# Hybrid decoder layer, the MLP's first matrix in quarters 1 to 3: seven half products in place of eight chunks

## The chip, the cores and the metric

The program runs on one core of one Trainium2 chip. The metric is device time in microseconds for one launch: the median of three runs is given, and one more execution is recorded by the hardware profiler. TensorE multiplies matrices, VectorE (DVE) and ScalarE (ACT) work element by element, GpSimd (POOL) and SyncE (SP) here mostly issue transfers, and 16 DMA engines carry them.

## The reference, cut to what matters

The layer computes a mixer, then an MLP, then a gated embedding. The MLP is

```python
u = rmsnorm(x, norm_mlp_g[i]) @ w_up[i]        # (512, 1024) @ (1024, 4096)
x = x + jnp.square(jax.nn.relu(u)) @ w_down[i] # (512, 4096) @ (4096, 1024)
```

All data are float32. Every product of two matrices is made of three products on TensorE: each factor is split into a high part, which is the factor rounded to the type fp32r, and a low part, the remainder; high by high, high by low and low by high are added in PSUM.

## The kernel before, in words

The 4096 hidden channels of the MLP are worked off in four quarters of 1024. In a quarter `up` makes the hidden values, transposed (channels on partitions, 512 tokens along the free dimension), and `down` multiplies them by the quarter's rows of the second matrix and adds the result to the residual rows `xk`.

`up` makes eight chunks of 128 channels. A chunk loads 512 KB of `w_up` into a buffer `wr`, forms its two parts `wh` and `wl` (`load_w`, `split`: a cast on ACT, then a subtraction on DVE), and runs 24 matmuls of 512 columns (8 slices of the inner dimension, three products each) into one PSUM bank `psg`. ACT applies relu and square. Two chunks give one tile `F` with the four blocks A21, A11, A22, A12 (two channel slices by two halves of the tokens) and four sums of them, S1 to S4, made on DVE. `F` is split into two tiles `uf`, high and low.

`down` is already made in Winograd's way: of the eight half products of a 2 by 2 block product it makes seven, from sums of the blocks on either side. Eight loads of 512 KB give the blocks b11, b12, b21, b22 for each half of the inner dimension; DVE makes sums of them in place; each of 14 forms is split and used in 12 matmuls of 512 columns into one of three PSUM pairs X, Y, Z (`psp`). The same seven products with 256 columns per matmul are used far earlier in the program, where the branch gates are projected (`gate_proj`; 24 matmuls per product).

The parts `wh` and `wl` each have four buffers (`WB = 4`), in rotation over the whole program: the parts of a product can be written as soon as the fourth product before it is done. `wr` has four buffers, `wd` (the first blocks of `down`) six, `F` one.

Another way of splitting stands in the program and is used for activations: `split_by_transfer` casts the high part on ACT, writes the negated high part into the low tile by a second ACT instruction with scale -1, and adds the source to it by an accumulating transfer between two places of SBUF, issued from POOL. DVE has no part in it.

```python
    def split_by_transfer(dst, src):
        A.copy(dst[0], src)
        A.activation(dst[1], src, AF.Copy, scale=-1.0)
        nc.gpsimd.dma_start(out=r32(dst[1]), in_=src, accum_op=ALU.add)
```

A scheduler places the instructions of each engine in one fixed order, by the order of the code and by when it reckons that their operands are there. On the chip each engine works its own list off in that order, and an instruction that waits on a semaphore holds up all that stands behind it.

## Time and profile before

| what | value |
|---|---|
| median of 3 runs | 879.4 us (878.7 to 879.86) |
| the profiled execution's own time | 878.13 us |
| its span, first to last instruction | 876.3 us |
| TensorE busy | 864.2 us (99%) |
| DVE busy | 671.5 us (77%) |
| ACT busy | 490.4 us (56%) |
| MLP, on the chain | 486.3 to 810.0 us |

The profile records one execution. "Busy" is the share of the span in which an engine has an instruction running; a matmul's own duration overlaps the next one's, so the pace of TensorE is read from the starts, not from the mean duration. The chain of waits is followed back from the last instruction: a stretch named PE in it is time in which TensorE itself sets the pace. Line numbers are those of the kernel before unless the text says otherwise.

### The profile page before, as it was taken

How to read it: one execution, taken by the hardware profiler on the slowest of the kernel's cores; microseconds unless marked ns; L12 is line 12 of the kernel's file. 1: busy time of each engine (PE TensorE's matmuls, PEld its weight loads, DVE VectorE, ACT ScalarE, POOL GpSimd, SP SyncE). 2: the span in 40 equal slices, each digit the busy share in tenths (PEclk: the TensorE clock that was granted, in tenths of full speed). 3: DMA queues.
4: the chain of work that ended last, by engine and by line, in shares of the span. 5: the costliest groups of instructions: out<-in, count | busy, mean ns of one | idle time of the engine just before them, and what ended most of it. 6: DMA issues, size and time to landing. Idle time of an engine off the chain costs nothing.

```text
span 876.3 us, 11735 instructions
## 1 busy us (share of the span) xinstructions
PE 864.2 (99%) x4428; PEld 727.1 (83%) x4428; DVE 671.5 (77%) x994; ACT 490.4 (56%) x826; POOL 43.7 (5%) x70
## 2 busy tenths in 40 slices
PE   9999999999999999999999999999999999999996
PEld 7888789998877778888888888888888888888886
DVE  6999889775788889777896669757956784698557
ACT  6685556444676568854344665356435634564843
POOL 1121111000000000000020000000000000020000
PEclk9999999999999999999999999999999999999999
DMA  8775246435121266664244612520452054125302
GB/s 268 209 185 207 97 148 209 146 115 202 49 97 50 72 231 215 209 254 148 73 88 148 222 47 73 204 106 4 135 178 73 0 192 145 49 54 139 120 1 96
DMA packets 35162, 115.14 MB, mean 131 GB/s; under 512 B 4893, under 2 KB 4893, under 8 KB 35106
## 3 DMA queue, kind: packets, MB, share of 16 engines
q1 hardware_dynamic: 28146, 95.25, 31.5%
q0 software_dynamic: 6816, 18.89, 7.9%
q8 instruction: 35, 0.57, 0.3%
q10 hardware_dynamic: 144, 0.26, 0.1%
q14 instruction: 21, 0.17, 0.1%
HBM read 97.60 MB, written 10.49 MB: 123 GB/s over the span
## 4 chain that ended last, share of the span: by engine, by line
PE 84%; DVE 7%; ACT 4%; DMA 3%; issue 2%; SPq 0%; ACTq 0%; DVEq 0%
PE psg L175 47%; PE psp L175 23%; PE psa L175 5%; DVE wl L138 2%; PE pst L175 2%; PE pst L778 1%; ACT wh L137 1%; DMA wr<-in_w_vsif 1%; DMA wq<-in_w_o 1%; ACT lm L743 1%; PE psa L720 1%; PE psa L859 1%; PE psa L881 1%; DVE qs L429 1%; PE psa L879 1%
## 5 line engine op out<-in xcount | busy, mean ns | idle before, releaser
L137 ACT CAST wh<-wr 128x1024 fp32r<-128x1024 f32 x130 | 136.5, 1052 | 159.4 <-PE psg L175 61.7
L138 DVE TENSOR_TENSOR wl<-wr,wh 128x1024 fp32r<-128x1024 f32 x130 | 158.1, 1219 | 79.9 <-ACT wh L137 78.9
L175 PE MATMUL psg<-x,wh 128*128 128x512 f32 x512 | 157.7, 389 | 0.0
L175 PE MATMUL psp<-wh,uf 128*128 128x512 f32 x448 | 138.5, 389 | 0.0
L175 PEld LDWEIGHTS psg<-x,wh 128*128 128x128 f32 x512 | 96.1, 188 | 19.9
L175 PE MATMUL psg<-x,wl 128*128 128x512 f32 x256 | 99.6, 389 | 0.0
L175 PEld LDWEIGHTS psp<-wh,uf 128*128 128x128 f32 x448 | 84.1, 188 | 17.4
L175 PE MATMUL psp<-wl,uf 128*128 128x512 f32 x224 | 87.1, 389 | 0.0
L175 PE MATMUL psg<-h,wh 128*128 128x512 f32 x256 | 80.9, 395 | 0.6 <-DVE rc L746 0.6
L137 ACT CAST wh<-wd 128x1024 fp32r<-128x1024 f32 x44 | 46.2, 1052 | 54.1 <-PE psp L175 21.9
L138 DVE TENSOR_TENSOR wl<-wd,wh 128x1024 fp32r<-128x1024 f32 x44 | 53.1, 1218 | 14.6 <-ACT wh L137 14.5
L175 PEld LDWEIGHTS psg<-x,wl 128*128 128x128 f32 x256 | 48.1, 188 | 9.9
L175 PEld LDWEIGHTS psg<-h,wh 128*128 128x128 f32 x256 | 46.9, 188 | 11.2 <-issue 1.6
L175 PE MATMUL psg<-h,wl 128*128 128x512 f32 x128 | 50.5, 395 | 0.0
L138 DVE TENSOR_TENSOR uf<-F,uf 128x1792 fp32r<-128x1792 f32 (+2 forms) x20 | 33.0, 1652 | 21.8 <-ACT uf L137 21.8
L175 PEld LDWEIGHTS psp<-wl,uf 128*128 128x128 f32 x224 | 42.1, 188 | 8.9
L175 PE MATMUL psg<-yb,wh 128*128 128x512 f32 x128 | 40.3, 393 | 0.0
L175 PE MATMUL psg<-ya,wh 128*128 128x512 f32 x128 | 39.9, 391 | 0.0
L137 ACT CAST uf<-F 128x1792 fp32r<-128x1792 f32 (+2 forms) x20 | 27.9, 1396 | 20.5 <-DVE F L1191 20.4
L1215 DVE SCALAR_TENSOR_TENSOR xk<-psp,r,xk 128x512 f32<-128x512 f32 x48 | 33.8, 744 | 5.5 <-PE psp L175 5.2
L175 PE MATMUL psg<-hS,wh 128*128 128x256 f32 x192 | 35.6, 285 | 0.2 <-DVE t L646 0.2
L175 PE MATMUL psa<-h,wh 128*128 128x256 f32 x192 | 35.4, 285 | 0.3 <-ACT p L656 0.2
(343 smaller groups left out, 1828.4 us busy)
## 6 DMA issues: line engine op xcount, KB each, us to landing
wr<-in_w_up SPq DMA_DIRECT2D x32, 512.0 KB, 3.3
wd<-in_w_down SPq DMA_DIRECT2D x24, 512.0 KB, 4.0
wr<-in_w_qsw SPq DMA_DIRECT2D x8, 512.0 KB, 4.2
gd<-gr POOLq DMA_DIRECT2D x8, 512.0 KB, 2.9
wr<-in_w_qkml SPq DMA_DIRECT2D x8, 512.0 KB, 3.2
wr<-in_w_b SPq DMA_DIRECT2D x8, 512.0 KB, 3.2
wh<-in_w_b POOLq DMA_DIRECT2D x8, 512.0 KB, 3.7
gl<-gd SPq DMA_DIRECT2D x8, 512.0 KB, 4.3
```

The source lines that it names most:

```text
L137: A.copy(dst[0], src)
L138: last_low[0] = V.tensor_sub(dst[1], src, r32(dst[0]))
L175: last_mm[0] = T.matmul(ps, l, r, start=first and i == 0, stop=last and i == len(ops) - 1, skip_group_check=parts)
L429: V.tensor_sub(t[o, :], ps[s, :], r32(t[s, :]))
L720: T.matmul(o, q[:, n * P : (n + 1) * P], kk[kp][ab][:, k0 : k0 + 256], start=True, stop=False)
L743: A.activation(lm3[:, g, :], lm3[:, g, :], AF.Exp, bias=nmx[:, g : g + 1], scale=0.125, accum_out=sm[:, g : g + 1])
L778: T.matmul(o[HALF[ab], :], v[:, c : c + 64], w[:, ab * 512 : (ab + 1) * 512], start=j == 0, stop=j == len(terms) - 1)
L859: T.matmul(psc[s], l, r, start=j == 0, stop=j == 2, skip_group_check=True)
L879: T.matmul(o, hi, vm[s][:, h, :], start=s == 0, stop=False, skip_group_check=True)
L881: last_mm[0] = T.matmul(o, lo, vm[s][:, h, :], start=False, stop=s == t, skip_group_check=True)
L1215: V.scalar_tensor_tensor(o, ps[:, t, :], r2[:, 2 * toks + t : 2 * toks + t + 1], o, ALU.mult, ALU.add)
```

## The change

Quarter 0 keeps its eight chunks (`up`). In quarters 1 to 3 `up_seven` takes their place. It works in two groups of 512 channels. A group loads four blocks of 512 KB (`four`, `_groups` lays `w_up` out for it), and makes seven products into three PSUM pairs, each of 24 matmuls with 256 columns: A11, A12, S2, S1, S3, S4, A22, named for the block or sum of the activations in it. Five sums of the weight blocks are made in place on DVE. The three forms for A11, A12 and S2 are split as before; the four for S1, S3, S4 and A22 are split by transfer. The seven results are put together on DVE with one copy `kept` of A11, then relu and square follow on ACT. The tile `F` now holds one whole group (two channel tiles) in one buffer, and S3 is written over A21.

The sums of the activations (S1 to S4 of x1) are made once, during quarter 0's `up`, on DVE and ACT (`x1_sums`). In `down`, the forms for S3, A22 and S4 are split by transfer in quarters 1 and 2 (`BY_DMA`); its blocks use four `wd` and four `wr` buffers, shared in turn with `up_seven`, and its first loop does the work of both halves one after the other. The scratch for transfer descriptors is set to 8192 bytes.

```diff
--- before.py
+++ after.py
...
+BY_DMA = (1, 2)
...
-    def load_w(src, n, dims, raw=None, cast=False):
+    def load_w(src, n, dims, raw=None, cast=False, how=None):
...
-            split(parts, raw[:, :n])
+            (how or split)(parts, raw[:, :n])
...
-    F = lambda: mp.tile([P, 8, 256], F32, tag="F", bufs=1, name=nm("F"))
-
-    A21, A11, A22, A12, S1, S2, S3, S4 = range(8)
+    F = lambda: mp.tile([P, 2, 7, 256], F32, tag="F", bufs=1, name=nm("F"))
+
+    A21, A11, A22, A12, S1, S2, S4 = range(7)
+    S3 = A21
...
+    def four(src, first):
+        tiles = []
+        for i in range(4):
+            if first:
+                t = np_.tile([P, 1024], F32, tag="wd", bufs=4, name=nm("wd"))
             else:
                 t = wp.tile([P, 1024], F32, tag="wr", bufs=WRB, name=nm("wr"))
-            nc.sync.dma_start(out=t, in_=w_down[q * 8 + c])
-            raws.append(t)
-        return raws
+            nc.sync.dma_start(out=t, in_=src[i])
+            tiles.append(t)
+        return tiles
...
+        q = {n: [r32(t) for t in v] for n, v in quad.items()}
+        add, sub = ALU.add, ALU.subtract
+        s1 = total((q["21"][0], add, q["22"][0]), (add, q["21"][1]), (add, q["22"][1]))
+        s2 = total((s1, sub, q["11"][0]), (sub, q["11"][1]))
+        parts("S2", s2)
+        s3 = total((q["11"][0], sub, q["21"][0]), (add, q["11"][1]), (sub, q["21"][1]))
+        parts("S3", s3)
+        s4 = total((q["12"][0], sub, s2), (add, q["12"][1]))
+        parts("S4", s4)
+
+        def last():
+            split(quad["21"], s1)
+            xsum["S1"] = x1_of(0, 0)
+            xsum["A11"], xsum["A12"], xsum["A22"] = x1_of(0, 256), x1_of(4, 256), x1_of(4, 0)
+
+        return last
...
+    def sums_of(f, cols):
+        V.tensor_add(f[S1], f[A21], f[A22])
+        V.tensor_sub(f[S2], f[S1], f[A11])
+        V.tensor_sub(f[S4], f[A12], f[S2])
+        V.tensor_sub(f[S3], f[A11], f[A21])
...
+    def up_seven(q, uf):
+
+        for g in range(2):
+            c = 8 + ((q - 1) * 2 + g) * 4
+            b11, b12, b21, b22 = four(w_up[c : c + 4], g == 0)
+            X, Y, Z = [pair()[:, :, :256] for _ in range(3)]
+            both = F()
+            f = [both[:, :, i, :] for i in range(7)]
+            kept = mp.tile([P, 2, 256], F32, tag="kp", bufs=1, name=nm("kp"))
+            hl = [new_uf() for _ in range(2)]
+
+            def form(raw, how=None):
+                return load_w(None, 1024, 4, raw, how=how)
+
+            def prod(ps, name, w, first, last):
+                for t in range(2):
+                    ops = []
+                    for k in range(4):
+                        ops += pairs([h[:, k, t * P : (t + 1) * P] for h in w], xsum[name][k])
+                    chain(ps[:, t, :], ops, first, last, True)
+
+            prod(X, "A11", form(b11), True, False)
+            A.copy(kept, X)
+            V.tensor_sub(b12, b22, b12)
+            V.tensor_add(b11, b12, b11)
+            prod(X, "A12", form(b21), False, True)
+            squared(f[A11], X)
+            V.tensor_sub(b21, b21, b11)
+            prod(Z, "S2", form(b11), True, False)
+            V.tensor_sub(b11, b22, b11)
+            V.tensor_add(f[A21], Z, kept)
+            prod(Z, "S1", form(b11, split_by_transfer), False, False)
+            V.tensor_add(f[A22], Z, kept)
+            prod(Y, "S3", form(b12, split_by_transfer), True, False)
+            V.tensor_add(f[A22], Y, f[A22])
+            squared(f[A22], f[A22])
+            prod(Z, "S4", form(b22, split_by_transfer), False, True)
+            V.tensor_add(f[A12], Z, kept)
+            squared(f[A12], f[A12])
+            if g:
+                for t in range(2):
+                    split([h[:, 256 : 4 * 256] for h in hl[t]], flat(both[:, t], 1, 4))
+            prod(Y, "A22", form(b21, split_by_transfer), False, True)
+            V.tensor_add(f[A21], Y, f[A21])
+            squared(f[A21], f[A21])
+            sums_of(f, 512)
+            for t in range(2):
+                if g:
+                    split([h[:, 4 * 256 :] for h in hl[t]], flat(both[:, t], 4, 7))
+                    split([h[:, :256] for h in hl[t]], flat(both[:, t], 0, 1))
+                else:
+                    split(hl[t], flat(both[:, t], 0, 7))
+                uf.append(hl[t])
...
-        raws = load_down(q)
+        raws = four(w_down[q * 8 : q * 8 + 4], True) + four(w_down[q * 8 + 4 : q * 8 + 8], False)
         b11, b12, b21, b22 = [[raws[4 * kh + i] for kh in range(2)] for i in range(4)]
         X, Y, Z = pair(), pair(), pair()
-
-        def form(raw):
-            return load_w(None, 1024, 2, raw)
+        by_dma = split_by_transfer if q in BY_DMA else None
+
+        def form(raw, how=None):
+            return load_w(None, 1024, 2, raw, how=how)
...
-            prod(Y, S3, form(b12[kh]), kh, False, False)
+            prod(Y, S3, form(b12[kh], by_dma), kh, False, False)
         acc(Y, 0, 1)
         for kh in range(2):
             V.tensor_sub(b11[kh], b22[kh], b11[kh])
             prod(Z, S1, form(b11[kh]), kh, True, False)
         acc(Z, 0, 1)
         for kh in range(2):
-            prod(Y, A22, form(b21[kh]), kh, False, True)
+            prod(Y, A22, form(b21[kh], by_dma), kh, False, True)
         acc(Y, 0, 0)
         for kh in range(2):
-            prod(Z, S4, form(b22[kh]), kh, False, True)
+            prod(Z, S4, form(b22[kh], by_dma), kh, False, True)
...
-        up(q, uf)
+        (up_seven if q else up)(q, uf)
...
-        "w_up": _t_form(i["w_up"][0]),
+        "w_up": np.concatenate([_t_form(i["w_up"][0][:, :1024]), _groups(i["w_up"][0][:, 1024:])], axis=0),
...
-    nc = _bacc.Bacc("TRN2", target_bir_lowering=False, num_devices=1)
+    nc = _bacc.Bacc("TRN2", target_bir_lowering=False, num_devices=1, dynamic_dma_scratch_size=8192)
```

Two places of the program show what the change makes of the order. The first is VectorE where quarter 2's `up` begins. In these rows `wl<-wd` or `wl<-wr` is the low part of a weight form, L1215 adds a product of `down` to the residual. Before:

```order
L138 TENSOR_TENSOR wl_6050<-wr_6047,wh_6049 128x1024
L1215 SCALAR_TENSOR_TENSOR xk_4163<-psp_5799,r_4939,xk_4163 128x512
L1215 SCALAR_TENSOR_TENSOR xk_4164<-psp_5799,r_4939,xk_4164 128x512
L138 TENSOR_TENSOR wl_6085<-wr_6082,wh_6084 128x1024
L138 TENSOR_TENSOR wl_6127<-wr_6124,wh_6126 128x1024
L1215 SCALAR_TENSOR_TENSOR xk_4165<-psp_5800,r_4939,xk_4165 128x512
L1215 SCALAR_TENSOR_TENSOR xk_4166<-psp_5800,r_4939,xk_4166 128x512
L138 TENSOR_TENSOR wl_6162<-wr_6159,wh_6161 128x1024
L138 TENSOR_TENSOR wl_6204<-wr_6201,wh_6203 128x1024
```

After, at the same place (L1275, L1276, L1279 and L1281 are the sums of the weight blocks, `wd_6256` to `wd_6262` the first group's b11, b12, b21, b22, `wr_6501` the second group's b12, L1327 the addition to the residual, `wl_6305` the low part for A12 and `wl_6336` that for S2, L1282 the first use of a result):

```order
L1275 TENSOR_TENSOR wd_6258<-wd_6262,wd_6258 128x1024
L139 TENSOR_TENSOR wl_6305<-wd_6260,wh_6304 128x1024
L1276 TENSOR_TENSOR wd_6256<-wd_6258,wd_6256 128x1024
L1275 TENSOR_TENSOR wr_6501<-wr_6505,wr_6501 128x1024
L1327 SCALAR_TENSOR_TENSOR xk_4165<-psp_6004,r_4939,xk_4165 128x512
L1327 SCALAR_TENSOR_TENSOR xk_4166<-psp_6004,r_4939,xk_4166 128x512
L1279 TENSOR_TENSOR wd_6260<-wd_6260,wd_6256 128x1024
L139 TENSOR_TENSOR wl_6336<-wd_6256,wh_6335 128x1024
L1281 TENSOR_TENSOR wd_6256<-wd_6262,wd_6256 128x1024
L1282 TENSOR_TENSOR F_6267<-psp_6266,kp_6268 128x2x256
```

Where the splits of independently loaded chunks stood between the additions, there now stand sums that feed each other. The source of the form for S1 is written by L1281; the second group's b12, both additions and the split for S2 stand ahead of it.

The second place is ScalarE in the second group of quarter 2. Before, in the middle of that quarter's `up` (relu, square, the cast of a chunk, and the cast of `F`):

```order
L1174 ACTIVATE rt_6112<-psg_6081 128x512
L1178 ACTIVATE F_6079<-rt_6112 128x512
L137 CAST uf_6115<-F_6079 128x1792
L137 CAST wh_6280<-wr_6278 128x1024
L1174 ACTIVATE rt_6154<-psg_6123 128x512
L1178 ACTIVATE F_6156<-rt_6154 128x512
L137 CAST wh_6315<-wr_6313 128x1024
L1174 ACTIVATE rt_6189<-psg_6158 128x512
L1178 ACTIVATE F_6156<-rt_6189 128x512
L137 CAST uf_6192<-F_6156 128x1792
```

After, from the last relu and square of the first group on (`wh_6608` and `wl_6609` are the two parts for the second group's S1, `wh_6638` and `wl_6639` those for its S3, `kp` the copy of A11, `uf` the cast of the first group's `F`, L147 the copy with scale -1 after which the transfer can be issued):

```order
L1219 ACTIVATE F_6267<-F_6267 128x2x256
L1220 ACTIVATE F_6267<-F_6267 128x2x256
L146 CAST wh_6608<-wr_6499 128x1024
L1274 COPY kp_6511<-psp_6507 128x512
L147 ACTIVATE wl_6609<-wr_6499 128x1024
L146 CAST wh_6638<-wr_6501 128x1024
L138 CAST uf_6269<-F_6267 128x1792
L147 ACTIVATE wl_6639<-wr_6501 128x1024
L138 CAST uf_6271<-F_6267 128x1792
```

The copy of A11 and one cast of `F` now stand between the casts and the scaled copies of S1 and S3.

More of the change, by code (lines that the diff above doesn't have):

```diff
@@ L1167, in up @@
         for f in range(8):
-            if q == 0 and f < 2:
+            if f < 2:
                 ps = begun[f]
@@ L1179, in up @@
-            if q == 0 and f == 2:
+            done = squared(flat(fs, o, o + 2), ps)
+            if f == 2:
                 with tc.issue_after(done.ins):
                     squares()
+                    last = x1_sums()
             if f % 2:
-                hl = [np_.tile([P, 7 * 256], F32R, tag="uf", bufs=8, name=nm("uf")) for _ in range(2)]
-                cut = 3 * 256 if f == 7 else 0
-                if cut:
-                    split([t[:, :cut] for t in hl], fs[:, 1:4, :].rearrange("p a b -> p (a b)"))
-                V.tensor_add(fs[:, S1, :], fs[:, A21, :], fs[:, A22, :])
-                V.tensor_sub(fs[:, S3, :], fs[:, A11, :], fs[:, A21, :])
-                V.tensor_sub(fs[:, S2, :], fs[:, S1, :], fs[:, A11, :])
-                V.tensor_sub(fs[:, S4, :], fs[:, A12, :], fs[:, S2, :])
-                split([t[:, cut:] for t in hl], fs[:, 1 + cut // 256 :, :].rearrange("p a b -> p (a b)"))
-                uf.append(hl)
+                hl = new_uf()
+                if f == 7:
+                    split([t[:, 256 : 4 * 256] for t in hl], flat(fs, 1, 4))
+                sums_of([fs[:, i, :] for i in range(7)], 256)
+                if f == 7:
+                    split([t[:, 4 * 256 :] for t in hl], flat(fs, 4, 7))
+                    split([t[:, :256] for t in hl], flat(fs, 0, 1))
+                else:
+                    split(hl, flat(fs, 0, 7))
+                uf.append(hl)
@@ L1228, in down @@
             V.tensor_sub(b12[kh], b22[kh], b12[kh])
-        for kh in range(2):
             w = form(b11[kh])
```

46 lines of the change are left out of this document (33 added, 13 removed).

## The prediction, made blind

> **What bounds the kernel now.** I read the page first, then the chain of waits, the waits of TensorE, and the busy time by stage.
>
> ```profile
> span 876.3 us, 11735 instructions
> ...
> PE 864.2 (99%) x4428; PEld 727.1 (83%) x4428; DVE 671.5 (77%) x994; ACT 490.4 (56%) x826; POOL 43.7 (5%) x70
> ...
> PEclk9999999999999999999999999999999999999999
> ```
>
> TensorE is busy in nearly the whole span, at full clock in every slice. The chain says how tightly:
>
> ```profile
> 176.61 2.88 PE psa L175 x24
> 179.49 2.88 PE psg L175 x24
> ...
> 565.20 43.52 PE psg L175 x192
> 608.72 38.08 PE psp L175 x168
> 646.80 43.52 PE psg L175 x192
> 690.32 38.08 PE psp L175 x168
> 728.40 43.52 PE psg L175 x192
> 771.92 38.11 PE psp L175 x168
> ```
>
> Columns are start, length, and number of instructions. Each `up` is one stretch of 43.52 us, each `down` one of 38.08 us, with nothing between. A 512-column matmul costs 43.52/192 = 0.2267 us, so a half product of `down` (12) takes 2.72 us. The first two rows are the gate projection, the same seven products with 256 columns: 24 matmuls in 2.88 us, 0.120 us each, a little over half.
>
> ```profile
> PE psg L267 <- DVE zero L215: 1.1, 1, 1.1
> ...
> 122.00:203.00 81.00, 80.44 (x665) 79.21 (x664) 66.02 (x89) 42.72 (x52) 7.33 (x13) 1.00 0.44 157
> ...
> 646.80:690.30 43.50, 43.50 (x193) 36.03 (x193) 25.30 (x29) 21.55 (x26) 0.00 (x0) 1.00 0.22 74
> 690.30:728.40 38.10, 38.10 (x170) 31.56 (x169) 33.09 (x35) 17.50 (x18) 0.00 (x0) 1.00 0.40 138
> ```
>
> The first row is TensorE's longest wait of the run, 1.1 us at the start. The others are stretches: window, length, then busy PE, PEld, DVE, ACT, POOL, clock, DMA share. In quarter 2's `up` DVE (25.3 of 43.5 us) and ACT (21.6) have room; in `down` DVE has little (33.1 of 38.1). The gate projection kept TensorE full (80.4 of 81) with ACT half idle and no transfers in its splits.
>
> **The change, part by part.** Prices, from the groups and the transfer views:
>
> ```profile
> L137 ACT CAST wh<-wr 128x1024 fp32r<-128x1024 f32 x130 | 136.5, 1052 | 159.4 <-PE psg L175 61.7 <-PE psp L175 48.0 <-issue 17.3
> L137 ACT CAST uf<-F 128x1792 fp32r<-128x1792 f32 x12 | 20.3, 1696 | 18.8 <-DVE F L1191 18.8
> L1178 ACT ACTIVATE F<-rt 128x512 f32<-128x512 f32 x32 | 20.3, 633 | 7.4 <-DVE uf L138 6.8
> L1174 ACT ACTIVATE rt<-psg 128x512 f32<-128x512 f32 x32 | 18.9, 589 | 1.2 <-PE psg L175 1.2
> L882 ACT COPY hs<-psa 128x512 f32<-128x512 f32 x8 | 4.3, 575 | 2.2 <-PE psa L881 2.2
> L1150 ACT ACTIVATE junk<-xk 128x1024 f32<-128x1024 f32 x4 | 4.2, 1046 | 0.0
> ...
> L138 DVE TENSOR_TENSOR wl<-wr,wh 128x1024 fp32r<-128x1024 f32 x130 | 158.1, 1219 | 79.9 <-ACT wh L137 78.9 <-PE psg L175 0.8
> L1215 DVE SCALAR_TENSOR_TENSOR xk<-psp,r,xk 128x512 f32<-128x512 f32 x48 | 33.8, 744 | 5.5 <-PE psp L175 5.2
> L138 DVE TENSOR_TENSOR uf<-F,uf 128x1792 fp32r<-128x1792 f32 x12 | 24.3, 2025 | 21.8 <-ACT uf L137 21.8
> L747 DVE TENSOR_TENSOR lm<-lm,rc 128x512 f32<-128x512 f32 x16 | 11.0, 689 | 0.4
> L1232 DVE TENSOR_TENSOR wd<-wd,wd 128x1024 f32<-128x1024 f32 x8 | 9.7, 1217 | 0.0
> L648 DVE TENSOR_TENSOR t<-psa,t 128x512 f32<-128x512 f32 x8 | 5.5, 686 | 1.4 <-PE psa L175 1.4
> ...
> DMA  0000089979999999999999996000000000000007
> ...
> q0 software_dynamic: 864, 1.57, 52.9%
> ...
> wr<-in_w_up SPq DMA_DIRECT2D x32, 512.0 KB, 3.3
> ...
> hS<-s POOLq DMA_DIRECT2D x8, 256.0 KB, 4.2
> ...
> DMA to landing us min/median/max: 3.2/4.2/7.4
> ...
> DMA to landing us min/median/max: 3.3/5.5/7.5
> ```
>
> *TensorE's saving.* An `up` goes from 192 x 0.2267 = 43.52 us to 14 x 2.88 = 40.32 us: 3.2 us a quarter, 9.6 us in all. That is the whole gain.
>
> *Work that must hide.* Per group TensorE has 7 x 2.88 = 20.2 us. ACT gets 7 casts (7.4), 4 scaled copies (4.2, by the 1.046 of an ACTIVATE of that size), the copy of A11 (0.6), 4 relus and squares (4.9), 2 casts of `F` (3.4): 20.5 us. DVE gets 5 sums (6.1), 3 splits (3.7), 5 additions from PSUM (3.4), 4 sums of `F` (2.8), 2 splits of it (4.1): 20.1 us. Both are as full as TensorE, with lists in fixed order; a wait of one is not made up inside the group.
>
> *The price of a remainder by transfer.* The last two rows are 256 KB adding transfers (L147, and `xk<-p1s` of L1225): 3.2 and 3.3 us from issue to landing when least disturbed. The DMA row above them covers 783 to 800 us in 40 slices of 0.425 us: six such transfers fill 20 slices, 1.4 us each. The change moves 512 KB, not shown here: 3.3 + 1.4 = 4.7 us alone, and up to 7.5 + 1.4 = 8.9 in a queue. I take L = 5.0, near the low end, since the gating ones are issued singly. Each also needs cast and scaled copy, 2.1 us: 7.1 us against 3 x 2.88 = 8.6 us from a buffer's release to its use. It fits only if ACT starts at once.
>
> *Start of quarters 2 and 3* (time 0 = end of the preceding `down`). A form there may begin when the product four earlier is done. S4's first transfer waits for S1's first half, which ends 5 x 2.72 = 13.6 us before 0; + 2.1 + 5.0 = -6.5. Only then may b22 be loaded into that buffer: + 3.3 = -3.2. DVE then works its row: b12 -2.0, split for A12 -0.8, b11 0.4, the second group's b12 1.7, two additions 3.1, b21 4.4, split for S2 5.6, source of S1 6.8. ACT: cast 7.9, relu of A12's result (queued ahead) 8.5, scaled copy 9.5; landing at 14.5. TensorE reaches the first matmul that needs it at 3 x 2.88 + 0.24 = 8.9. **Wait 5.6 us**, twice = 11.2. In quarter 1 no transfer delays the loads: additions 1.5, split for S2 2.7, source 3.9, scaled copy 6.0, landing 11.0 against 9.1: 1.9.
>
> *Second group* (0 = end of the first group's A22). DVE's last addition 0.7, relu and square 1.9, cast for S1 3.0, copy of A11 3.6, scaled copy 4.6, cast for S3 5.7, cast of `F` 7.4, scaled copy 8.4, landing 13.4. S3's first low part is wanted at 8.9: 4.5 us, in quarters 2 and 3 = 9.0. In quarter 1 the cast of `F` stands behind the scaled copy: landing 11.8, wait 2.9. Even without it `F`, with one buffer, would hold S1: casts and splits of `F` end at 12.2, the first addition into it at 12.9, where S1 is wanted at 9.2.
>
> *`down` of quarters 1 and 2.* The second S3 cast stands ahead of the first scaled copy and waits for S2's second half. Quarter 2: 10.9, cast 11.9, scaled copy 13.0, landing 18.0; wanted at 6 x 2.72 + 0.45 = 16.8: 1.2 us. In quarter 1 S2's second half is placed among A12's matmuls, ends near 13.4, landing 20.5, wanted at 18.0: 2.5 us. The other four remainders have 8.2 us and fit.
>
> *Priced at nothing.* x1's sums in quarter 0 add 10 + 4 DVE operations (17 us) to a stage with 25.3 of 43.5 busy; cover gone, up to +2. `down` of quarter 3 keeps 33.1 of 38.1 us of DVE but starts late behind `F`'s splits: up to +3. Transfers: 36 x 1.4 x 2 = 101 us of DMA time in 240, beside loads at a share of 0.21 to 0.40, so room on average. POOL and SP have nothing else queued that TensorE waits for.
>
> *Sum.* -9.6 + 11.2 + 1.9 + 9.0 + 2.9 + 1.2 + 2.5 = +19.1; 878.1 + 19.1 = **897.2 us**, against the profiled execution (878.13; the median is 879.4).
>
> The Trainium skill ("DMA: Bandwidth & Descriptors", "Anatomy of one DMA") fits 2.0 us plus bytes over 436 GB/s to a transfer of this path, 3.2 us for 512 KB by my estimate; by it the sum would be near 883, where `F`'s single buffer holds instead. The rows disagree with it, 3.2 us being the least for half the bytes, so I go by the rows.
>
> **Rivals.** *All hidden.* DVE and ACT run further ahead than my rows allow, and landings come in time: 878.1 - 9.6 = 868.5; if ACT's 20.5 and 21 us per group set the pace, about 872. For it: the gate projection did hide its forms (80.4 of 81). Against: there ACT had 42.7 us in 81, here 41 in 40. It decides if S1's remainder in quarter 2 is issued 5.6 us earlier than 9.5. 0.18.
>
> *Slow clock after long waits.* Waits of 4.5 to 5.6 us are longer than any of before (1.1), with the clock at 9 throughout. If the clock halved after each of the four, and stayed so for one product, 4 x 2.88 = 11.5 us: 908.7. No row here speaks for it. 0.12. The Trainium skill ("TensorE: Matmul & The Clock Gate", "Why this matters for your kernels") warns that a gap above about 3 us drops TensorE to half clock; no run here shows one.
>
> *Half hidden.* The six waits of the two `up` places shrink to a third because loads and casts run earlier: 25.0/3 + 3.7 - 9.6 = +2.4, 880.5. 0.08.
>
> My forecast has 0.62.
>
> **Numbers.** The forecast's own range is 888 (the 28.7 us of waits a third shorter) to 907 (L = 6, with quarters 2 and 3 paying it twice, +10). Over all cases I give 871 to 912: about 0.12 lies below, 0.06 above. Below 0.2%, about 1.8 us, a measurement of this kernel can't tell a change. Faster 0.19, same 0.02, slower 0.79.
>
> **What would show it.** `up` of quarters 2 and 3 as several stretches with gaps of about 5 us at S1 of the first group and S3 of the second, TensorE waiting there for a transfer into `wl`; 24 matmuls still in 2.88 us; adding transfers of 512 KB landing in about 5 us; `down` of quarter 3 without gaps. Wrong would be: one unbroken stretch of 40.3 us per `up`; landings near 3 us; or a granted clock below 9 behind the gaps.

## The result, and the profile after

The changed kernel takes 961.0 us (median; 959.9 to 965.9) where the kernel before takes 879.4 on the same chip: 1.094 times as long, 95% interval 1.090 to 1.098. That is 82 us slower, where 19 were forecast. The page of its profiled execution (959.9 us):

```profile
span 958.1 us, 12853 instructions
...
PE 886.4 (93%) x4860; PEld 756.8 (79%) x4860; DVE 711.0 (74%) x1030; ACT 547.6 (57%) x900; POOL 74.2 (8%) x106
...
PEclk9999999999999999999999899899998998989999
...
q0 software_dynamic: 12000, 37.76, 17.7%
```

TensorE was busy in nearly all of the span before and now in 93% of it. Its granted clock, 9 in every slice before, is 8 in five slices of the second half. The queue of GpSimd's transfers carries 37.8 MB in 12000 packets (18.9 in 6816 before) and takes 17.7% of the DMA engines' time, 7.9% before. The stretches below hold the whole MLP, then each quarter in two parts, quarters 0 to 3 (`up`, in quarters 1 to 3 with the first three half products of `down`, and the long wait behind them; then the rest of `down`); the columns are window, length, then busy PE, PEld (TensorE's weight loads), DVE, ACT, POOL, the clock, the DMA share and GB/s.

```profile
481.30:891.80 410.50, 353.06 (x1905) 303.55 (x1903) 280.24 (x310) 226.00 (x269) 35.63 (x42) 0.93 0.51 134
481.30:541.80 60.50, 51.59 (x235) 41.91 (x232) 48.66 (x65) 36.17 (x50) 0.00 (x0) 0.97 0.28 93
541.80:579.20 37.40, 37.24 (x157) 30.46 (x158) 32.98 (x33) 16.37 (x16) 0.00 (x0) 0.95 0.34 113
579.20:642.90 63.70, 53.30 (x374) 50.07 (x372) 40.79 (x43) 41.46 (x49) 7.59 (x9) 0.95 0.55 133
642.90:679.60 36.70, 33.02 (x133) 25.67 (x134) 20.14 (x25) 16.10 (x18) 4.23 (x5) 0.95 0.78 198
679.60:749.00 69.40, 54.91 (x373) 51.28 (x371) 42.06 (x45) 41.16 (x50) 6.78 (x8) 0.90 0.49 122
749.00:788.00 39.00, 35.11 (x133) 26.67 (x134) 23.35 (x27) 17.25 (x19) 5.07 (x6) 0.91 0.73 189
788.00:856.40 68.40, 53.98 (x373) 50.81 (x371) 40.99 (x44) 41.40 (x50) 6.76 (x8) 0.92 0.50 123
856.40:891.80 35.40, 33.92 (x134) 26.68 (x135) 31.27 (x35) 16.10 (x20) 5.21 (x6) 0.91 0.57 149
```

The same work before is one window without a gap:

```profile
481.60:810.00 328.40, 328.40 (x1459) 272.13 (x1459) 238.44 (x271) 166.95 (x192) 5.20 (x6) 1.00 0.33 109
```

So the MLP went from 328.4 to 410.5 us, +82.1, which is the whole loss. It divides in two. TensorE **waits** 410.5 - 353.1 = 57.4 us. And it is **busy** 353.1 us, where 328.4 - 9.6 = 318.8 would do: 34.3 us more for the same products. The sum is -9.6 + 57.4 + 34.3 = +82.1. The waits by what ended them, between 480 and 895 us (us in total, times, longest):

```profile
PE psp L176 <- DMA wl<-wr: 17.6, 5, 5.6
PE psp L176 <- DMA wl<-wd: 12.1, 11, 2.5
PE psp L176 <- ACT wh L138: 8.2, 3, 7.5
PE psp L176 <- ACT uf L138: 5.1, 2, 2.9
PE psp L176 <- ACT wh L146: 4.3, 2, 2.4
...
PE psp L176 <- DVE p L1349: 2.8, 1, 2.8
```

Half of them, 29.7 us, end with an adding transfer (`wl<-wr`, `wl<-wd`). One wait of 7.5 us is in quarter 0, for the cast of a form of `down`; the waits for `uf` and `p` come three half products, 8.3 us, into the later `down`s.

The other 34 us are seen behind the waits. The next two rows are stretches right behind the wait of 5.6 us in quarter 2, which ended at 725.07.

```profile
725.10:729.60 4.50, 4.49 (x21) 4.49 (x22) 0.00 (x0) 0.60 (x2) 0.85 (x1) 0.50 1.07 300
729.70:737.90 8.20, 8.20 (x71) 8.20 (x70) 4.00 (x5) 4.20 (x5) 0.00 (x0) 1.00 0.65 187
```

At clock 0.50 a 256-column matmul takes 4.49/21 = 0.214 us, then 0.116. Ten such stretches of 3.4 or 6.8 us lie in the MLP, none before. Summed matmul by matmul in the trace, they hold some 21 us more than the same matmuls at full clock. Of the remaining 13 us, some 7 are waiting too: a matmul's record is 0.28 us long while the starts lie 0.12 apart, so at each of the 39 waits the tail of the last record counts as busy. Some 5 us more lie in 56 starts that are late without any idle time.

### The profile page after: what moved, and what is told of

Same layout as the page of the kernel before. It is cut to its first block, busy times and chain, and to the rows that moved or that the text cites. A ratio compares the mean times of both kernels' runs of the same rounds, so it can differ in the third digit from the quotient of the medians.

```text
span 958.1 us, 12853 instructions
## 1 busy us (share of the span) xinstructions
PE 886.4 (93%) x4860; PEld 756.8 (79%) x4860; DVE 711.0 (74%) x1030; ACT 547.6 (57%) x900; POOL 74.2 (8%) x106
## 3 DMA queue, kind: packets, MB, share of 16 engines
q0 software_dynamic: 12000, 37.76, 17.7%
## 4 chain that ended last, share of the span: by engine, by line
PE 46%; DMA 11%; DVE 9%; ACT 8%; issue 5%; POOL 0%; POOLq 0%; DVEq 0%; ACTq 0%; SPq 0%
PE psg L176 23%; PE psp L176 16%; DMA wl<-wd 5%; DMA wl<-wr 2%; DVE wl L139 2%; ACT wl L147 1%; ACT wh L146 1%; PE pst L779 1%; DMA wd<-in_w_up 1%; DMA wd<-in_w_down 1%; DVE xk L1327 1%; ACT uf L138 1%; PE psa L176 1%; ACT wh L138 1%; DMA wr<-in_w_up 1%
## 5 line engine op out<-in xcount | busy, mean ns | idle before, releaser
L176 PE MATMUL psp<-x,wh 128*128 128x256 f32 x384 | 77.1, 301 | 2.5 <-ACT kp L1274 1.9
L176 PEld LDWEIGHTS psp<-x,wh 128*128 128x128 f32 x384 | 65.8, 210 | 3.8 <-ACT kp L1274 2.7
L176 PE MATMUL psp<-x,wl 128*128 128x256 f32 x192 | 58.2, 303 | 7.0 <-DMA wl<-wd 7.0
L176 PE MATMUL psp<-xh,wh 128*128 128x256 f32 x288 | 56.0, 294 | 4.9 <-ACT wh L146 4.3
L176 PE MATMUL psp<-xh,wl 128*128 128x256 f32 x144 | 43.5, 302 | 17.1 <-DMA wl<-wr 14.4
L176 PEld LDWEIGHTS psp<-xh,wh 128*128 128x128 f32 x288 | 47.5, 202 | 5.6 <-ACT wh L146 4.8
L139 DVE TENSOR_TENSOR wl<-wd,wh 128x1024 fp32r<-128x1024 f32 x31 | 37.8, 1219 | 15.6 <-ACT wh L138 15.5
L176 PEld LDWEIGHTS psp<-x,wl 128*128 128x128 f32 x192 | 40.0, 208 | 8.3 <-DMA wl<-wd 8.3
L176 PEld LDWEIGHTS psp<-xh,wl 128*128 128x128 f32 x144 | 29.4, 204 | 18.7 <-DMA wl<-wr 15.0
L1327 DVE SCALAR_TENSOR_TENSOR xk<-psp,r,xk 128x512 f32<-128x512 f32 x48 | 33.7, 745 | 12.9 <-PE psp L176 12.9
L139 DVE TENSOR_TENSOR uf<-F,uf 128x768 fp32r<-128x768 f32 (+2 forms) x30 | 33.6, 1149 | 10.7 <-ACT uf L138 10.7
```

Of the source, the lines that this page charges most:

```text
L139: last_low[0] = V.tensor_sub(dst[1], src, r32(dst[0]))
L176: last_mm[0] = T.matmul(ps, l, r, start=first and i == 0, stop=last and i == len(ops) - 1, skip_group_check=parts)
L1327: V.scalar_tensor_tensor(o, ps[:, t, :], r2[:, 2 * toks + t : 2 * toks + t + 1], o, ALU.mult, ALU.add)
```

## The experiments

Times are medians of three or more rounds. The kernel before took 878.8 to 879.0 in them; the changed one stands at its 961.0. A profile is of one execution, which can lie a few us off the median.

**What is the half clock worth?** `stalls` is the kernel before with three waits put in, ahead of `down` in quarters 1, 2 and 3 (and the matmuls of these quarters kept in written order):

```diff
+    def stall(n):                       # n = 1, 3, 6
+        a = last_a[0]
+        for i in range(n):
+            b = mp.tile([P, 512], F32R, tag="rt", bufs=3, name=nm("st"))
+            nc.gpsimd.tensor_copy(b, a)
+            a = b
+        tc.keep_in_program_order(T.matmul(ps_g(), a[:, :P], a, start=True, stop=True))
```

> The kernel before, with one wait of TensorE put between up and down in each of quarters 1, 2 and 3 and nothing else: a matrix product that nobody reads, which needs a chain of 1, 3 and 6 copies on the idle GpSimd after the last relu of up. By about 0.7 us a copy the waits are some 2, 4 and 6 us. What is asked is what a wait costs beside its own length. Theory (the clock is halved behind a long wait): behind the second and third wait the granted clock is 0.5 for 3.4 or 6.8 us and the time above 878.9 is the sum of the three waits plus 3 to 7 us. Rival (the half clock of the changed kernel came from something else, its smaller products or its DMA traffic): clock 1.00, and the time above 878.9 is the sum of the waits within 1 us.

899.3 us, 20.5 above the kernel before. The waits in its profile, and stretches behind each of them (2.64, 4.14 and 6.84 us):

```profile
PE psg L183 <- POOL st L180: 13.6, 3, 6.8
```

```profile
612.30:617.00 4.70, 4.70 (x14) 3.71 (x15) 3.03 (x5) 1.24 (x2) 0.00 (x0) 0.64 0.00 0
617.10:640.00 22.90, 22.90 (x102) 18.94 (x102) 20.37 (x20) 9.42 (x9) 0.00 (x0) 1.00 0.37 119
700.20:705.80 5.60, 5.60 (x13) 4.39 (x14) 2.26 (x3) 1.04 (x1) 0.00 (x0) 0.50 0.00 0
791.80:798.00 6.20, 6.20 (x15) 4.85 (x16) 1.08 (x1) 0.30 (x1) 0.00 (x0) 0.50 0.25 85
```

The waits make 13.6 us, the total is 6.9 more, and 9.2 more in the profiled execution (901.6): some 2.3 to 3.1 us behind each wait, nearly all half clock, in an MLP without 256-column matmuls or adding transfers of weights. The theory holds. The Trainium skill ("TensorE: Matmul & The Clock Gate", "Why this matters for your kernels") sets the gap at about 3 us; here 2.64 us was enough.

**What do the transfers cost?** Three kernels: `down_dve` takes them out of `down`, `no_transfers` out of `up` too, and `add_on_dve` keeps ACT's scaled copy and lets DVE do the addition. (The edit of `add_on_dve`, like that of `on_pool` below, stands in the helper, so it also takes the eight smaller transfers of the gate projection; the MLP begins 0.9 and 2.4 us later in their traces than in that of the changed kernel.)

```diff
-BY_DMA = (1, 2)
+BY_DMA = ()                                             # down_dve, no_transfers
-            prod(Z, "S1", form(b11, split_by_transfer), False, False)
+            prod(Z, "S1", form(b11), False, False)      # no_transfers; S3, S4, A22 too
-        nc.gpsimd.dma_start(out=r32(dst[1]), in_=src, accum_op=ALU.add)
+        last_low[0] = V.tensor_add(dst[1], src, r32(dst[1]))   # add_on_dve
```

> The changed kernel with all remainders of down made by DVE, as before the change; the transfers stay in up alone. Theory (transfers that queue behind one another are late in down): the five waits of down for a transfer, 0.82 + 1.42 + 1.43 in quarter 1 and 0.96 + 1.83 in quarter 2, go, with one stretch of half clock, and the time falls from 961.0 to about 954 (951 to 957). Rival (DVE has no room in down, where it would be busy 38 to 40 us of some 50): as slow or slower, 960 to 966.

> The changed kernel with all remainders made by DVE, none by a transfer, in up and in down. DVE then has 20.1 + 4 x 1.22 = 25.0 us a group beside 20.2 us of TensorE, ACT 16.3. Theory (it is the lateness of transfers, not the seven products, that costs most): no wait for wl by a transfer; DVE's 4.8 us too many are paid in each of the six groups, 29 us, in short waits without half clock; below the kernel with transfers in up alone (948.4), at about 940 (933 to 947). Rival (DVE as the pace costs more than the transfers): 950 to 975.

> The changed kernel with ACT's cast and scaled copy as they are, and each of the 36 adding transfers replaced by the same addition on DVE. ACT then has what it has with transfers (20.5 us a group), DVE what it has with none (25.0). Theory (the lateness of transfers made the difference of 43 us between 961.0 and 917.8): 918 to 925. Rival (ACT's scaled copies, 1.05 us each, made it, since ACT's queue holds TensorE): 935 to 955.

948.4, 917.8 and 918.8 us; the first two are lower than their theories. So, DVE's added work already paid, the 12 transfers of `down` cost 12.6 us and all 36 cost 43.2, and it isn't ACT's scaled copies, which `add_on_dve` still makes. With DVE's list at 25.0 us a group, `no_transfers` was expected to pay 29 us in `up`. Its waits for DVE's remainders make 1.9 us, and the long waits are others:

```profile
PE psp L176 <- ACT F L1219: 10.7, 3, 3.6
PE psp L176 <- ACT uf L138: 8.6, 3, 2.9
PE psp L176 <- ACT wh L138: 7.6, 2, 7.5
PE psp L176 <- DVE wl L139: 1.9, 4, 0.8
```

Three waits of 3.6 us are for `F`, which has one buffer, at the second group; three of 2.9 for the last `uf`, early in `down`; one of 7.5 is in quarter 0. The transfers had stood in front of the first kind.

**Quarter 0's wait: work or a buffer?** `s1_in_p1` moves one tile of x1's sums; `dve_s1` does the same in `no_transfers`.

```diff
-        s1 = total((q["21"][0], add, q["22"][0]), (add, q["21"][1]), (add, q["22"][1]))
+        s1 = total(..., t=p1.rearrange("p a (k c) -> p (a k) c", k=2))    # not a wd buffer
```

> The changed kernel with one tile moved: the sum S1 of x1, made in quarter 0, is kept in p1 (unused until the end of quarter 0's down) and not in one of the four wd buffers. Theory (a buffer, not work): S1's sum holds its wd buffer until the last matrix product of quarter 0's up, so the fourth w_down tile of kh = 0 is loaded late and TensorE waits 7.45 us at 534.36 with half clock behind it; with the tile moved this wait falls below 2 us and the time from 961.0 to about 952 (950 to 954). Rival (DVE is overloaded in quarter 0 by the 14 added operations, 17 us): the wait stays above 5 us and the time at 958 to 961.

> All remainders by DVE, and S1's sum of x1 kept in p1. Theory (the two causes are independent): the wait of 7.46 us at the start of quarter 0's down goes, with about 2 us of half clock, 917.8 to about 908 (906 to 911). Rival (quarter 1 waits for what quarter 0 no longer waits for): 913 to 918.

952.6 (8.4 less) and 907.8 (10.1 less). The wait of 7.5 us is gone in both, although DVE does the same 14 operations. `s1` held a `wd` buffer until the last matmul of quarter 0's `up` (533.1 in the changed kernel's trace), and only then, at 533.1, does the load of the fourth tile of `w_down` go out. The overloaded DVE of the rival is ruled out.

**Is each lateness of its own?** `low_last` puts the matmuls that read the low part last; `in_order` keeps `up`'s matmuls in written order; `on_pool` gives the remainders to GpSimd; `filler` puts unread matmuls ahead of the waits.

```diff
-                        ops += pairs([h[:, k, t * P : (t + 1) * P] for h in w], xsum[name][k])
+                        ops += [(wk[1], a[0])] if low else [(wk[0], a[0]), (wk[0], a[1])]   # low_last: low = 0 for both t, then 1
+            if kept_order[0]: tc.keep_in_program_order(last_mm[0])                          # in_order
-        A.activation(dst[1], src, AF.Copy, scale=-1.0)
-        nc.gpsimd.dma_start(out=r32(dst[1]), in_=src, accum_op=ALU.add)
+        nc.gpsimd.tensor_sub(dst[1], src, r32(dst[0]))                                      # on_pool
+            if g == 1: stir((22, 42, 42)[q - 1])        # filler, ahead of S3; 32 ahead of S1 (g = 0, q > 1)
```

> The changed kernel with the order of the matrix products inside each product of up and down turned: all that read the high part of the weights first, those that read the low part last. In up the low part is then wanted 14 x 0.12 = 1.7 us later, in a half product of down 6 x 0.227 = 1.4 us later. Theory (each wait for a transfer is a lateness of its own): the fifteen waits for wl, 25.9 us, shrink by 12.7 us in up and 5.9 us in down, with some half clock: 961.0 to about 940 (935 to 946). Rival (the chain of casts, transfers and buffers sets the pace, so that what is won at one product is waited for at the next): 952 to 961.

> The changed kernel with the matrix products of up in quarters 1 to 3 kept in the order in which they are written. As it stands, six products of S3 of the second group, with one that reads S3's low part, stand ahead of all 24 of S1 on TensorE, so S1, whose transfer has landed 4.6 us earlier (720.49 against 725.07), waits with S3. Theory (the order on TensorE adds to the wait): the waits of the second group, 3.2, 5.6 and 5.6 us, are each shorter by up to 2.9 us: 961.0 to about 952 (950 to 955). Rival (S1 itself would be late, or the following product is): 958 to 962.

> The changed kernel with the 36 remainders made by GpSimd's subtraction of the cast from the source, in place of a scaled copy on ACT and an adding transfer. ACT loses 4.2 us a group. Its time for 128x1024 is not known here; by a cast of 128x792 in 0.77 us at least 1.0 us, by twice DVE's time 2.4 us. Theory (what costs is the transfer's 4.4 to 10 us from issue to landing): the waits for wl, 25.9 us, and a part of the half clock go, to 925 (915 to 935). Rival (GpSimd and DVE hinder each other, so that what GpSimd does is lost on DVE, 4 x 1.2 to 2.4 us a group or more): DVE's own operations get longer in the profile and the time is 940 to 990.

> The changed kernel with matrix products that nobody reads put in front of the five longest waits of up (22 and twice 42 ahead of S3 of the second group in quarters 1, 2, 3; 32 ahead of S1 of the first group in quarters 2 and 3), to keep TensorE busy while it would wait. Theory (the half clock behind a wait is a cost of its own, about 2 us at each): the granted clock stays at 1.00 at these places, the transfers land as before, and the time falls from 961.0 to about 950 (947 to 954). Rival (the clock costs nothing, since the next wait is for a transfer or an engine that does not run with that clock): 959 to 963. If the filler overshoots the waits, up to 2 us more in either case.

`low_last`: 942.8, 18.3 less. That is the theory's number, but only in part its reason: in its profile (an execution of 947.3) the waits for a transfer fall from 29.7 to 20.0 us, half of the 18.6 expected, other waits grow, and less half clock makes some 4 us. `in_order`: 959.8, as the rival had it. The waits of the second group did shrink (`wl<-wr`, 17.6 before), and others took their place:

```profile
PE psp L177 <- DMA wl<-wd: 15.5, 9, 4.2
PE psp L177 <- ACT kp L1277: 10.4, 6, 2.8
...
PE psp L177 <- DVE F L1285: 5.1, 4, 1.4
...
PE psp L177 <- DMA wl<-wr: 3.9, 3, 1.8
```

`on_pool`: 946.3, the rival's side. Almost no wait for GpSimd is left, but its subtractions take 2.4 to 4.1 us, DVE's sums of `F` beside them up to 2.0 (0.69 in `dve_s1_f_tail`, where GpSimd has none), and `F` is late by 6.9:

```profile
PE psp L175 <- DVE F L1281: 20.8, 3, 6.9
...
PE psp L175 <- POOL wl L147: 2.5, 2, 1.2
```

```profile
L1207 DVE TENSOR_TENSOR F<-F 128x512 f32<-128x512 f32 x5 | 9.7, 1936 | 0.1
```

`filler` leaves the question of the clock open: 969.5, slower than both expectations. In quarter 2 some ten of S3's matmuls stood ahead of S1 and of the filler; TensorE waited there for S3's transfer (2.5 us), and the filler, 5.2 us, came behind it and covered no wait. `stalls` is what answers it.

All the mended places together, `four_mended` (`s1_in_p1`, `down_dve`, `low_last` and `in_order`):

> The changed kernel with four edits together: S1's sum of x1 in p1, the remainders of down by DVE, the low parts read last, and the products of up in their written order. Theory (the causes are independent): 961.0 - 8.4 - 12.6 - 18.3 - 8 = about 914 (908 to 924). Rival (the second group's chain over ACT and the one buffer F holds the end of up wherever the transfers land): 925 to 940. Both stay above the 878.9 of the kernel before.

942.0 us, no better than `low_last` alone. Its waits:

```profile
PE psp L177 <- ACT uf L138: 14.9, 3, 5.0
PE psp L177 <- ACT kp L1281: 13.6, 6, 6.8
PE psp L177 <- DVE F L1289: 9.0, 5, 3.8
PE psp L177 <- DMA wl<-wd: 6.6, 6, 1.7
```

What each edit won alone doesn't add. With the transfers nearly on time TensorE waits for ACT's copies and `F` instead. The rival was right in kind; the time lies just above its 925 to 940.

**What is left without transfers?** `dve_s1_f_tail` is `dve_s1` with S1 and S4 summed in two free PSUM banks (no wait for `F`), `in_order`, and S1's first half in `down` ahead of what needs the second group (for which A22's source there takes one more operation on DVE).

```diff
-            prod(Z, "S1", form(b11), False, False)
+            W = [ps_g()[:, :256] for t in range(2)]
+            prod(W, "S1", form(b11), True, False)          # f[A22] = W + f[A21]; S4 into W too
+            if kh == 0:                                    # in down, behind S2
+                V.tensor_sub(b11[0], b22[0], b11[0])
+                prod(Z, S1, form(b11[0]), 0, True, False)
```

> All remainders by DVE, S1's sum of x1 in p1, and against the two waits that are left in each of quarters 1 to 3, 3.6 us for F at the second group and 2.9 us at the start of down: S1 and S4 are summed in two free banks of PSUM, so that S1 need not wait for the first addition into F; up's products keep their written order; down takes S1's half of the first group (k half 0) before those that need the second group's outputs. Theory (these waits and the half clock behind them are what is left): 908 - 3 x 6.4 - about 8 of half clock = 881 (876 to 888). Rival (DVE, 25 us a group beside 20.2 of TensorE, is the pace and the waits only move): 893 to 908.

890.4 us, between the two expectations. The first row is its quarter 2, the next its waits:

```profile
651.50:735.70 84.20, 80.26 (x507) 71.60 (x506) 80.06 (x88) 45.44 (x54) 0.00 (x0) 1.00 0.32 100
```

```profile
PE psp L177 <- DVE wl L139: 6.6, 10, 2.7
PE psp L177 <- ACT kp L1280: 6.2, 6, 1.5
```

No wait over 2.7 us is left, here the clock is 1.00, and the quarter takes 84.2 us where before it took 81.6 (43.5 + 38.1). DVE is busy in 80.1 of them. In the whole MLP TensorE still waits 13.5 us, half of it for DVE's low parts and half for ACT's copy `kp`: more than the 9.6 us saved.

Read one behind the other, the transfers cost 43.2 us, the buffer of `s1` 10.1, the three things mended here 17.4, and 11.6 are left. Since gains don't add, another order of the edits could divide them differently.

**One transfer a group.** In that kernel, S1's remainder alone (`s1_transfer`) or A22's alone (`a22_transfer`) again by a transfer:

```diff
-            prod(W, "S1", form(b11), True, False)
+            prod(W, "S1", form(b11, split_by_transfer), True, False)
```

> The kernel of dve_s1_f_tail (890.4) with S1's remainder alone, in each of the six groups, made by ACT's scaled copy and an adding transfer: one transfer a group, no burst, at the place where the sum is ready last. DVE loses 1.2 us a group. Theory (even one transfer alone, 4.4 us from issue to landing, comes too late where its source is made shortly before its product): S1 waits for wl in each group, 2 to 4 us and half clock behind some: 900 to 915. Rival (only bursts are late; a single transfer fits into the three products of lead): 884 to 891.

> The kernel of dve_s1_f_tail (890.4) with A22's remainder alone, in each of the six groups, made by ACT's scaled copy and an adding transfer: one transfer a group, at the place where the source is ready earliest before its product. Theory (alone and with time to spare a transfer is hidden, and DVE's 1.2 us a group come free): no wait for wl by a transfer, 883 to 890. Rival (the buffers of wh and wl, four each, let it start only three products ahead whatever its source does, so it is late here too): 892 to 905.

906.1 and 898.4: 15.7 and 8.0 us dearer than without. The theory holds for S1 and falls for A22. Issue to landing (least, median, most) of the six in `s1_transfer`, of the six in `a22_transfer`, and of the eight of quarter 1's `up` in the changed kernel:

```profile
DMA to landing us min/median/max: 4.3/4.6/4.8
```

```profile
DMA to landing us min/median/max: 4.6/5.6/8.0
```

```profile
DMA to landing us min/median/max: 4.4/6.3/9.0
```

S1's transfers land in the time they take alone, and TensorE still waits for three of them, 1.9, 3.2 and 3.9 us: the source is made too late. In quarter 2 DVE ends S1's sum at 660.9, the transfer goes out at 664.07 behind cast, relu and scaled copy, and TensorE wants it at 665.31. A22's run beside the loads of `w_down`, and two land after 6.9 and 8.0 us, for which TensorE waits 1.4 and 2.6 us; with the 4.6 us of the quickest they would have been in time (669.2 against 670.05, 757.7 against 758.69). In the changed kernel, the four of a group land after 4.4, 4.9, 7.1 and 9.0 us (quarter 1, first group), each behind the one ahead.

**Can DVE be relieved?** In the same kernel, `dve_pool` gives A22's source to GpSimd and puts A12 behind S2 in `up`; `a12_third` does the second alone; `a12_early` saves one DVE operation in each `down`; `both_and_ple` does both and moves the split of p's rows.

```diff
-            V.tensor_sub(b21, b21, b11)
+            G.tensor_sub(b21, b21, b22)            # dve_pool; + S1's source later, on GpSimd too
-            prod(X_, "A12", form(b21), False, True)
             prod(Z_, "S2", form(b11), True, True)
+            prod(X_, "A12", form(b21), False, True)   # a12_third
+                w12 = form(b21[0])                 # a12_early, in down ahead of S1's first half
+                V.tensor_sub(b21[0], b21[0], b11[0])
```

> The kernel of dve_s1_f_tail (890.4) with A22's source made by GpSimd in place of DVE (b21 - b22, and then + S1's source, so that no later sum waits for it), in up and in down, and with A12's product of up behind S2's, so that the copy of A11 has 2.9 us. Theory (what is left is DVE's work and the wait for that copy): DVE loses 1.2 us a group and 3.7 us a down, the waits of 0.7 + 1.2 to 1.5 us for the copy go, and the time is 876 (871 to 881), near or below the 878.8 of the kernel before. Rival (GpSimd's subtractions, 2.4 to 2.8 us each, come late for A22 or hold DVE up): 886 to 900.

> The kernel of dve_s1_f_tail (890.4) with A12's product of up behind S2's, so that the copy of A11 out of PSUM, for which TensorE waits 0.7 and 1.2 to 1.5 us in each of quarters 1 to 3, has 2.9 us. Theory (DVE, busy 80.1 of 84.2 us in a quarter, is the pace, and the waits for the copy are only where TensorE is held): 888 to 891. Rival (the waits are a cost of their own): 883 to 885.

> The kernel of dve_s1_f_tail (890.4) with the form of A12 (first k half) of down ahead of S1's, so that A22's source needs one DVE operation and not two: one operation of 1.22 us less in each down, nothing else. Theory (DVE is the pace): 4 x 1.2 us less, 885 to 887. Rival (it is not): 889 to 891.

> Both edits (A12 third in up, A12's form early in down), and the split of p's rows, two operations on ACT and DVE, moved behind the last down, where TensorE waits 2.7 us for a remainder. Theory (DVE's work is what is left): DVE has some 79 us a quarter beside 78.4 of TensorE: 880 to 884, with the wait of 2.7 us and the half clock behind it gone; not below the kernel before (878.9). Rival (the seven products can pay on these engines): 870 to 877.

925.1, 895.1, 896.0 and 899.0: all slower than 890.4, none near 878.9, and each outside both of its expectations, which together reach from 870 to 900. Executions of one kernel lie up to 8.5 us apart here (`dve_pool` 920.8 to 929.2, `both_and_ple` 894.9 to 901.1), so the last three aren't ranked. In `dve_pool` the reason is in DVE's own rows (shape, count, busy, mean ns):

```profile
L139 DVE TENSOR_TENSOR wl<-wr,wh 128x1024 fp32r<-128x1024 f32 x38 | 58.2, 1531 | 1.7 <-ACT wh L138 1.7
...
L1287 DVE TENSOR_TENSOR wd<-wd,wd 128x1024 f32<-128x1024 f32 x3 | 7.0, 2335 | 0.0
```

Both take 1.22 us in `dve_s1_f_tail`, where GpSimd subtracts nothing. In `both_and_ple` (an execution of 894.9) quarter 2 reads, `up` and then `down`:

```profile
655.40:690.00 34.60, 34.60 (x290) 34.59 (x288) 32.08 (x34) 22.27 (x26) 0.00 (x0) 1.00 0.33 107
690.00:741.00 51.00, 45.69 (x219) 37.18 (x218) 48.03 (x55) 23.34 (x28) 0.00 (x0) 1.00 0.28 94
```

These 290 matmuls of `up` run without a gap, 34.6/290 = 0.119 us each, and what it wins is lost in `down`, where DVE is busy 48.0 of 51.0 us. That waits only move speaks for DVE as the pace; but `a12_early`, which takes 1.2 us from DVE in each `down` and was expected at 885 to 887, is 5.6 us slower. Its trace says where: TensorE is busy 13.4 us at half clock, against 3.3 in `dve_s1_f_tail`, which costs some 5 us; the stretches come behind waits of 1.58, 0.44 and 0.36 us close together. Without them, by this estimate, it would be about as fast as 890.4 and not faster, so DVE's operations alone aren't the pace. How the 11.6 us between 890.4 and 878.8 divide between DVE's work and the order of forms through four buffers stays open.

## Why the prediction was wrong

The direction and the main reason, remainders that land late, were right. The sum was 28.7 us of waits less 9.6; measured are 57.4 us of waits and 34.3 us of slower or late matmuls, less 9.6. So two steps failed: the half clock stood beside the sum as a rival and not in it (34.3 us more of busy TensorE, some 21 of them half clock), and the waits outside the two priced places of `up` were put at nothing or too low. Of the 28.7 us of waits too few, 6.3 lie inside `up`, 3.3 inside `down` of quarters 1 and 2, 9.1 in quarter 0, 7.9 early in the later `down`s, the rest in `down` of quarter 3 and in short gaps.

- *TensorE's saving, 9.6 us.* Right: 0.119 us a matmul in the gapless `up` above, 0.120 forecast.
- *The waits inside `up`, forecast at 25.0 us.* Nearly right. At S3 of the second group 4.5 us was forecast and 5.6 measured, twice (2.9 and 3.2 in quarter 1); at S1 of the first group 5.6 was forecast and 2.4 + 2.0 (quarter 2) and 2.0 + 2.5 (quarter 3) measured, the first of each for S1's cast on ACT and the second for the transfer. The waits over 0.35 us inside `up` sum to 31.3. The chain of the second group in quarter 2:

```profile
713.40 2.72 issue
...
716.17 0.81 POOL wl L148
716.98 2.63 issue
719.62 5.45 DMA wl<-wr
725.07 0.04 issue
725.11 9.91 PE psp L176 x64
```

S1's transfer goes out at 716.1 and lands at 720.5, S3's goes out at 719.6 behind cast, cast of `F` and scaled copy, the three that the prediction named. `F`'s hold behind it, forecast at 12.9 - 9.2 = 3.7 us, is the 3.6 of `no_transfers`.
- *L = 5.0 us, "since the gating ones are issued singly".* The number held where it was used in `up`: the gating transfers took 4.4 us at S1 and 5.4 to 5.5 at S3 of the second group, and alone they take 4.3 to 4.8 (4.7 was worked out). The reason didn't: a group's four go out within 6 to 9 us, and the last two take 5.7 to 9.9. The same slip is in "101 us of DMA time in 240 ... so room on average": the share is 1.07 of the engines behind the wait at 725. The 3.2 us estimated from the fit in the Trainium skill ("DMA: Bandwidth & Descriptors", "Anatomy of one DMA") is below every landing of these transfers.
- *"The other four remainders have 8.2 us and fit", `down` 1.2 + 2.5 us.* Wrong, and the wrong way round: the waits over 0.5 us inside `down` of quarters 1 and 2 sum to 7.0 us, five of the six for a transfer (6.5 us), and all five are at A22 and S4, the remainders that were to fit, whose transfers take 5.1 to 11.5 us from issue to landing. S3's, the two that were priced, land in 4.4 to 6.4 us, in time. `down_dve` puts the twelve at 12.6 us.
- *"Priced at nothing": x1's sums, "up to +2".* Wrong in size and cause: 7.5 us of wait, 8.4 to 10.1 of time by the two runs that move one tile. DVE's operations weren't it; the tile of `s1` kept a `w_down` load waiting. Of the sums the prediction counted the operations and not the buffers.
- *Early in `down`.* The prediction named "starts late behind `F`'s splits: up to +3" for quarter 3 and put it at nothing. TensorE waits there in all three quarters, 2.8, 2.2 and 2.9 us: in quarter 1 for DVE's addition `p` out of PSUM, which stands behind two splits and a sum of `F`, in quarters 2 and 3 for the last cast of `F`, which stands on ACT behind relu and square and three or two casts of weight forms.
- *Slow clock, a rival at 0.12 and 11.5 us.* This was the largest error. It isn't a rival but a part of every forecast with waits of this length: some 21 us at half clock, in ten stretches and not four. "No row here speaks for it" isn't so: in the trace of the kernel before the last matmul starts at 869.0, and from 872.1 to the end the granted clock is 0.50, which the digit of a 21.9 us slice rounds away. By the 2.3 us of `stalls`, the four to six long waits that the prediction itself named had to carry 9 to 14 us more, as a term of the sum.
- *All hidden, 868.5.* Ruled out by the 29.7 us of waits that end with a transfer. *Half hidden*, 880.5: ruled out too, as the 25.0 us in `up` came as 31.3 and not as a third.

Of what would show it right: `up` in several stretches, with TensorE waiting for a transfer into `wl` at S1 and S3, came true, as did 0.12 us a matmul at full clock; `down` of quarter 3 without gaps didn't (1.4 us for DVE's low part, besides the 2.9). Of the signs of being wrong, "a granted clock below 9 behind the gaps" is what came.

## What to carry to other kernels

A wait of TensorE is dearer than its length: in these runs one of 2 to 3 us and more mostly brought 2 to 3 us of half clock with it, which belongs into the sum. Where three engines are each as full as the time allows, price the buffers and the order of each queue, not only the operations: a tile that stays in a shared buffer cost 8 us here without any work of its own. And a product saved on TensorE pays only if the engines that prepare its operands have the time; here DVE's list grew until it was as long as TensorE's, and every way of relieving it that was run (one transfer a group, GpSimd, another order) made the best version slower, by 4.7 to 34.7 us.

## What the hardware showed that was not expected

- The half clock. It comes in stretches of 3.4, 6.8 or 10.2 us. 2.64 us sufficed in `stalls`, and 1.8 and 2.2 us once each in the changed kernel, while 2.9 us brought none early in `down` in `dve_s1`; 1.58 + 0.44 + 0.36 us close together brought one in `a12_early`, 1.80 + 0.45 + 0.36 none in two quarters of `both_and_ple`. So the length alone doesn't decide. In the changed kernel's trace the stretches begin whole multiples of 3.41 us apart (538.47, 616.98, 644.28 and 692.07 are 23, 8 and 14 steps), so it may matter where in a step a wait falls; no run varies that.
- GpSimd and DVE hold each other up. A GpSimd subtraction of 128x1024 takes 2.4 us at its best and up to 4.1, and DVE's of the same size rises from 1.22 us to a mean of 1.42 or 1.53 in `dve_pool`. The Trainium skill ("SBUF — State Buffer", "SBUF: two separate sides") states a lock on a port that the two share; the longer rows agree with it, though no run here shows the lock itself.
- Adding transfers of 512 KB: 4.3 to 4.8 us as the only one of a group (`s1_transfer`), and in the first groups of the changed kernel 4.4, 4.8 to 4.9, 7.1 to 7.9 and 9.0 to 9.9 us as a burst of four, beside the loads of `w_down`.
